# RWKV-7 recurrence of a hybrid decoder step: chunk by chunk, or solves and transition matrices in batches

## The chip, the core and the metric

The kernel runs on one core of a Trainium2 chip. The metric is the device time of one execution in microseconds, the median of the runs shown. TensorE (PE) multiplies, VectorE (DVE), ScalarE (ACT) and GpSimd (POOL) do the element-wise work and empty PE's accumulators (PSUM), SyncE (SP) issues most of the transfers. Beside the times there is one profiled execution, whose trace gives every instruction of every engine.

## What is computed

One layer for 256 prompt tokens and 64 sample tokens (8 sequences of 8): a combined projection, three branches, gates, an output projection and a convolutional GLU. The change is in the first branch, twelve heads of 64 with a delta rule per token:

```python
def _wkv7_step(S, inp):
    r, w, k, v, kk, a = inp
    sa = jnp.einsum('bhvk,bhk->bhv', S, -kk)
    S = S * w[:, :, None, :] + sa[..., None] * (kk * a)[:, :, None, :] + v[..., None] * k[:, :, None, :]
    return S, jnp.einsum('bhvk,bhk->bhv', S, r)
```

The outputs o are normalised per head, get a bonus term and a gate and go into the branch's projection. The final states are outputs too, one for the prompt and one for each sample sequence.

## The kernel before

All tokens stand side by side: 320 columns, 256 of the prompt and 64 of the samples. A large product (`step` at L365, `mm3` at L100) multiplies a weight block of 128x128, split into a high and a low part (`wh` cast by ACT at L361, `wl` subtracted by DVE at L362), with the activations, also split, in three matmuls over 320 columns: L101, L102, L103.

The recurrence works on six pairs of heads, `hp` 0 to 5, in ten chunks of 32 tokens: chunks 0 to 7 are the prompt, 8 and 9 hold four sample sequences each. With half a pair on 64 partitions, `early(hp)` (L487) forms decay, keys and queries, the triangular matrices `Tm` (L538), and the transposes `bkT`, `UV`, `arT` (L559 to L583). `inverse(hp)` (L604) inverts the triangular matrices on DVE and writes them to `IT` by way of DRAM. `late(hp)` (L645) does the recurrence proper. It begins with `PT` (L658), the product of the inverse with `arT`. Then `chunk` (L667) runs ten times. Its first burst multiplies `IT` with `UV` (L672) and adds the state's part (L677, for samples L675); ACT copies the result into `UV` (L678, L679). Its second burst forms the state's increment (L686), the outputs (L698) and the outputs' part from the state (L704, for samples L701); POOL scales the old state (L693) and DVE adds (L694). The four products at L722 give the samples' new states. At the end come the two output transfers, the copy of `pso`, and a tail that normalises and gates (L733 to L749).

The order on PE is written by a planner (`pump`, L387) with a clock of its own. In each turn it first lets every thread (`early`, `inverse`, `late`) go on whose delay has passed or whose condition holds, then it emits one `step` of the first large product in the list and moves its clock by 0.405; if no product may run, it moves the clock by 0.2 and emits none. A `yield` of a number is a delay on that clock, a `yield` of a function a condition. On PE the order of the program is kept; the other engines' instructions are ordered by the framework. The delays that matter: `HOP` = 1.2 after each burst of a chunk, `TRS` = 2.4 after batches of transposes, `NI_LAT`, `BLK_LAT` = 6, `IT_LAT` = 8 in the inverse. The conditions: `early(hp)` waits for `state["late"] >= hp - 1` (L515), the transfer into `IT` too (L636), and a `late` for the one before it (L646) and its inverse (L651).

The list of products: 2 low-rank inputs, then for each pair 3 columns (k, r, v) and `FILL` = 3, 2, 3, 2, 2, 2 others, each of 16 steps; then 16 gate columns, which may run only when `early` has reached 6 (L765, L768), because their output takes the place of early's tiles; then the branch's projection, which needs all six pairs' outputs (L782), and the attention stage.

## Time and profile before

| | us |
|---|---|
| runs: median (lowest, highest) of 3 | 2121.61 (2120.63, 2124.82) |
| profiled execution, span | 2120.2 |
| PE busy in the span | 2066.6 |
| stage with recurrence on PE | 170 to 571.5 |

The span is the time from the first to the last instruction of the profiled execution. A busy time is the union of an engine's instructions; matmuls are pipelined, so a PE that is busy throughout can still issue slowly. In a timeline of PE a line like `x4` stands for four records; a product of two f32 operands that are not of the split kind makes two records, one for each pass. The form `64*32` behind MATMUL gives the rows and columns of the array that it uses. Lines with `sm` and `pso` are small products, those with `bigps` large ones. The page's rows on DVE, ACT and POOL give their busy time; idle time of these costs only what PE waits for.

### The profile page before, as it was taken

Reading aid. Unit: us, or ns where it says so; the run is one execution under the profiler, and the core shown is the slowest. Engines: PE = TensorE matmul, PEld = TensorE weight load, DVE = VectorE, ACT = ScalarE, POOL = GpSimd, SP = SyncE. Lnnn points to the kernel's source line nnn. Section 1 sums busy time; section 2 is a strip of 40 time slices with the busy share of each in tenths; the row PEclk is TensorE's granted clock in tenths of the full one; section 3 lists DMA queues with packets and bytes.
Section 4 is the critical chain, followed back from the end, with each engine's and each line's share of the span. In section 5 each row is a group of like instructions: output and inputs, shape, how many; then the busy total and the mean of one; then the engine's idle time right before and its main releaser. Section 6 shows DMA issues by size and latency. Waiting matters only on the chain.

```text
span 2120.2 us, 37224 instructions
## 1 busy us (share of the span) xinstructions
PE 2066.6 (97%) x15250; PEld 1967.7 (93%) x15250; DVE 1224.8 (58%) x2052; ACT 830.2 (39%) x1372; POOL 255.1 (12%) x506
## 2 busy tenths in 40 slices
PE   8999999999999999999999999999999999999996
PEld 7888888878899889999998999999999999999995
DVE  7677667756356665444545754455555455455457
ACT  5543433432243343333444433343333333333234
POOL 4512232232110000000101300000000000000002
PEclk9999999989999999999999999999999999999998
DMA  7533332333265443554544244445444444444443
GB/s 269 170 120 102 116 107 89 106 97 95 86 225 162 134 127 121 157 159 147 195 159 149 97 149 150 149 152 188 150 149 154 150 149 151 149 149 150 149 138 109
DMA packets 92619, 303.39 MB, mean 143 GB/s; under 512 B 11164, under 2 KB 17078, under 8 KB 92432
## 3 DMA queue, kind: packets, MB, share of 16 engines
q1 hardware_dynamic: 83232, 273.49, 39.9%
q0 software_dynamic: 8496, 26.71, 3.9%
q8 instruction: 119, 1.95, 0.4%
q10 hardware_dynamic: 720, 0.82, 0.1%
q14 instruction: 52, 0.43, 0.1%
HBM read 293.59 MB, written 9.34 MB: 143 GB/s over the span
## 4 chain that ended last, share of the span: by engine, by line
PE 92%; DVE 4%; DMA 1%; issue 1%; ACT 1%; POOL 1%; SPq 0%; DVEq 0%; ACTq 0%; POOLq 0%
PE bigps L101 28%; PE bigps L102 26%; PE bigps L103 26%; PE sm L672 1%; PE sm L677 1%; PE sm L675 1%; PE sm L686 1%; PE sm L129 1%; PE sm L150 1%; DMA NI<-sc 1%; PE pso L698 0%; PE sm L590 0%; PE pso L701 0%; PE sm L852 0%; DVE wl L222 0%
## 5 line engine op out<-in xcount | busy, mean ns | idle before, releaser
L101 PE MATMUL bigps<-XH,wh 128*128 128x320 f32 x2680 | 856.3, 320 | 2.6 <-ACT XH L1069 1.7
L102 PE MATMUL bigps<-XL,wh 128*128 128x320 f32 x2680 | 830.5, 310 | 2.3 <-POOL XL L262 1.5
L103 PE MATMUL bigps<-XH,wl 128*128 128x320 f32 x2680 | 830.5, 310 | 2.1 <-DVE wl L362 2.1
L101 PEld LDWEIGHTS bigps<-XH,wh 128*128 128x128 f32 x2680 | 505.3, 189 | 18.2 <-issue 4.6
L97 DVE TENSOR_TENSOR wl<-raw,wh 128x1024 fp32r<-128x1024 f32 (+1 forms) x299 | 359.5, 1203 | 275.1 <-ACT wh L96 274.6
L102 PEld LDWEIGHTS bigps<-XL,wh 128*128 128x128 f32 x2680 | 505.8, 189 | 5.2 <-POOL XL L262 2.4
L96 ACT CAST wh<-raw 128x1024 fp32r<-128x1024 f32 (+1 forms) x299 | 306.3, 1025 | 517.3 <-PE bigps L102 406.5
L103 PEld LDWEIGHTS bigps<-XH,wl 128*128 128x128 f32 x2680 | 505.2, 188 | 2.6 <-DVE wl L362 2.6
L362 DVE TENSOR_TENSOR wl<-raw,wh 128x1024 fp32r<-128x1024 f32 (+2 forms) x212 | 243.2, 1148 | 180.9 <-ACT wh L361 179.5
L361 ACT CAST wh<-raw 128x1024 fp32r<-128x1024 f32 (+2 forms) x212 | 208.3, 983 | 329.8 <-PE bigps L102 259.3
L102 PE MATMUL bigps<-fl,wh 128*128 128x320 f32 x704 | 217.4, 309 | 0.0
L101 PE MATMUL bigps<-fh,wh 128*128 128x320 f32 x704 | 217.4, 309 | 0.0
L103 PE MATMUL bigps<-fh,wl 128*128 128x320 f32 x704 | 217.3, 309 | 0.0
L101 PEld LDWEIGHTS bigps<-fh,wh 128*128 128x128 f32 x704 | 132.1, 188 | 0.2 <-ACT fh L155 0.2
L102 PEld LDWEIGHTS bigps<-fl,wh 128*128 128x128 f32 x704 | 132.1, 188 | 0.1
L103 PEld LDWEIGHTS bigps<-fh,wl 128*128 128x128 f32 x704 | 132.1, 188 | 0.0
L1115 POOL COPY cout<-zp 128x9 f32<-128x9 f32 x88 | 16.5, 218 | 743.5 <-DVE zp L1112 743.5
L1141 DVE TENSOR_TENSOR yacc<-yacc,bigps 128x320 f32<-128x320 f32 x80 | 38.9, 487 | 84.6 <-PE bigps L103 84.5
L101 PE MATMUL bigps<-MG,wh 128*128 128x320 f32 x208 | 64.3, 309 | 0.0
L102 PE MATMUL bigps<-MG,wh 128*128 128x320 f32 x208 | 64.3, 309 | 0.0
L103 PE MATMUL bigps<-MG,wl 128*128 128x320 f32 x208 | 64.2, 309 | 0.0
L693 POOL TENSOR_SCALAR SP<-S,pc 128x64 f32<-128x64 f32 x42 | 36.3, 865 | 171.2 <-DVE S L694 144.4
(391 smaller groups left out, 2531.4 us busy)
## 6 DMA issues: line engine op xcount, KB each, us to landing
raw<-in_wup SPq DMA_DIRECT2D x176, 512.0 KB, 3.5
raw<-in_win SPq DMA_DIRECT2D x164, 512.0 KB, 3.6
raw<-in_wdn SPq DMA_DIRECT2D x80, 512.0 KB, 3.4
raw<-in_wo SPq DMA_DIRECT2D x32, 512.0 KB, 3.5
raw<-in_wbr_rw SPq DMA_DIRECT2D x16, 384.0 KB, 3.4
raw<-in_wbr_sw SPq DMA_DIRECT2D x16, 384.0 KB, 3.4
ck<-in_cmk POOLq DMA_DIRECT2D x8, 512.0 KB, 4.5
cv<-in_cmv POOLq DMA_DIRECT2D x8, 512.0 KB, 4.7
```

The source lines that it names most:

```text
L96: A.copy(out=h, in_=raw)
L97: V.tensor_sub(out=l, in0=raw, in1=h.bitcast(F32))
L101: PE.matmul(ps, h, xh, start=start, stop=False)
L102: PE.matmul(ps, h, xl, start=False, stop=False)
L103: PE.matmul(ps, l, xh, start=False, stop=stop)
L129: mm = PE.matmul(pst[:, nh * j:nh * j + nh], sq_[:, t0:t0 + 128], rhs, start=q == 0, stop=q == len(sqs) - 1)
L150: PE.matmul(ps[:, n:n + c1 - c0], lhs, C["ident"][:, c0:c1], start=True, stop=True)
L361: A.copy(out=h, in_=c[2])
L362: V.tensor_sub(out=l, in0=c[2], in1=h.bitcast(F32))
L672: PE.matmul(psu[us, 0:64], IT[us, c, :], UV[us, c, :], start=True, stop=c == 0)
L693: G.tensor_scalar(out=SP, in0=S, scalar1=pcc, scalar2=None, op0=ALU.mult)
L1141: V.tensor_add(out=yacc[:, m, :], in0=yacc[:, m, :], in1=ps)
```

## The change

The chunk loop goes. For a pair of heads, `late` now runs: (1) four matmuls for the samples' transition and the solves `IT` times [`arT` | `UV`] for chunks 8, 9 and 0 to 3, 128 columns at a time, (2) the solves of chunks 4 to 7 and the samples' state part, (3) for each chunk the product that gives its state transition (`AB`, block-diagonal for both heads, with the identity added) and the corrected queries, the state increments of all prompt chunks into one bank `psb`, and the outputs from `UV` into `pso`, (4) a chain of seven matmuls, each `AB` times the state, added in `psb` onto the increment, scaled by ACT into `SA`, (5) one closing group: outputs from the states, and the samples' new states. Delays of `SLV` = 2.4 stand behind (1) and (2), `HOP` behind (3) and between the links of the chain. `Tm` and `bkT` become one tile `BT`, `UV` and `arT` one tile `AU`; `ar` has its two halves exchanged, and the mask's columns follow. The two low-rank products of `early` are taken over all 128 partitions with zeros in the other half. The tail's products move from a bank of their own to the two of `early`. `S2` moves to another pool.

```diff
-ARTB = 1
+SLV = 2.4
...
-            tc.tile_pool(name="pso", bufs=1, space=PSUM) as psop, tc.tile_pool(name="ppo", bufs=1, space=PSUM) as ppo, \
+            tc.tile_pool(name="pso", bufs=1, space=PSUM) as psop, tc.tile_pool(name="psb", bufs=1, space=PSUM) as psbp, \
...
+        lord = rws.tile([128, T], F32, name="lord")
+        G.memset(lord[64:128, :], 0.0)
...
+        its = [rws.tile([128, 11, 32], F32, name=f"IT{j}") for j in range(2)]
...
+        AB = rws.tile([128, 7, 128], F32, name="AB")
+        G.memset(AB, 0.0)
+        PTz = rws.tile([128, 2, 64], F32, name="PTz")
+        G.memset(PTz, 0.0)
...
-                    A.activation(out=lora[0][0:64, :], in_=lora[0][0:64, :], func=AF.Tanh)
+                    A.activation(out=lord[0:64, :], in_=lora[0][0:64, :], func=AF.Tanh)
+                    G.memset(lora[0][0:64, :], 0.0)
...
-            PE.matmul(psz, lw[0:64, 0, cs], lwa[0:64, :], start=True, stop=True)
+            PE.matmul(psz, lw[:, 0, cs], lord, start=True, stop=True)
...
-            PE.matmul(psa, lw[64:128, 0, cs], lwa[64:128, :], start=True, stop=True)
+            PE.matmul(psa, lw[:, 0, cs], lora[0], start=True, stop=True)
...
-            Tm = rwm.tile([128, 10, 64], F32, tag="Tm", name="Tm")
+            BT = rwm.tile([128, 10, 128], F32, tag="BT", name="BT")
...
-            bkT = rwm.tile([128, 10, 64], F32, tag="bkT", name="bkT")
-            UV = rwm.tile([128, 10, 64], F32, tag="UV", name="UV")
-            arT = rwm.tile([128, 10, 64], F32, tag="arT", name="arT", bufs=ARTB)
+            AU = rwm.tile([128, 10, 128], F32, tag="AU", name="AU")
...
+        def late(hp, ar, pc, bonus, BT, it, AU):
             yield lambda: state["late"] == hp
             cs = slice(hp * 128, hp * 128 + 128)
             S0 = rw1.tile([128, 8, 64], F32, tag="S0", name="S0")
             nc.gpsimd.dma_start(out=S0, in_=i["wkv"][hp])
             yield lambda: it[0] is not None
+            ITf = it[0].rearrange("p c t -> p (c t)")
+            fss = [slice(64 * h, 64 * h + 64) for h in range(2)]
+            uss = [slice(64 * h, 64 * h + 32) for h in range(2)]
+
+            def bank():
+                return pch.tile([128, 512], F32, tag="sm", name="sm")
+
+            def solve(ps, lo, hi):
+                for c in range(lo, hi):
+                    for h in range(2):
+                        PE.matmul(ps[fss[h], 128 * (c - lo):128 * (c - lo) + 128], ITf[uss[h], 32 * c:32 * c + 64],
+                                  AU[uss[h], c, :], start=True, stop=True)
+
+            def solved(ps, lo, hi):
+                for h in range(2):
+                    (A.copy if h else V.tensor_copy)(out=AU[uss[h], lo:hi, :],
+                                                     in_=ps[uss[h], 0:128 * (hi - lo)].rearrange("p (c f) -> p c f", f=128))
+
+            ps1, ps2 = bank(), bank()
+            for cc in range(2):
+                for h in range(2):
+                    PE.matmul(ps1[fss[h], 256 + 32 * cc:288 + 32 * cc], AU[uss[h], 8 + cc, 0:64],
+                              it[0][uss[h], 8 + cc, :], start=True, stop=True)
+            solve(ps1, 8, 10)
+            solve(ps2, 0, 4)
+            A.copy(out=PTz[:, :, 0:32], in_=ps1[:, 256:320].rearrange("p (c t) -> p c t", t=32))
+            solved(ps1, 8, 10)
+            solved(ps2, 0, 4)
+            yield SLV
+            ps3 = bank()
+            solve(ps3, 4, 8)
+            solved(ps3, 4, 8)
+            psz = bank()
+            for cc in range(2):
+                for h in range(2):
+                    PE.matmul(psz[fss[h], 256 * cc:256 * cc + 256], PTz[fss[h], cc, :],
+                              S0[fss[h], 4 * cc:4 * cc + 4, :].rearrange("p s v -> p (s v)"), start=True, stop=True)
+            UVm = rw1.tile([128, 2, 4, 64], F32, tag="UVm", name="UVm")
+            V.tensor_add(out=UVm, in0=psz.rearrange("p (c s v) -> p c s v", s=4, v=64),
+                         in1=AU[:, 8:10, 64:128].unsqueeze(2).to_broadcast([128, 2, 4, 64]))
+            G.tensor_mul(out=UVm, in0=UVm, in1=C["smask"].unsqueeze(1).unsqueeze(3).to_broadcast([128, 2, 4, 64]))
+            yield SLV
+            for lo, hi in ((1, 5), (5, 10)):
+                ps = bank()
+                pv = ps[:, 0:480].rearrange("p (c f) -> p c f", f=96)
+                for c in range(lo, hi):
+                    w = 0 if c < 8 else 64
+                    for h in range(2):
+                        PE.matmul(pv[fss[h], c - lo, w:96], AU[uss[h], c, 0:64], BT[uss[h], c, w:96], start=True, stop=True)
+                n = min(hi, 8) - lo
+                for h in range(2):
+                    hs = slice(64 * h, 64 * h + 64)
+                    V.tensor_add(out=AB[hs, lo - 1:lo - 1 + n, hs], in0=pv[hs, 0:n, 0:64],
+                                 in1=C["ident"][hs, hs].unsqueeze(1).to_broadcast([64, n, 64]))
+                qv = ar[:, 0, 32 * lo:32 * hi].rearrange("p (c t) -> p c t", t=32)
+                V.tensor_add(out=qv, in0=pv[:, 0:hi - lo, 64:96], in1=qv)
+            psb = psbp.tile([128, 512], F32, tag="psb", name="psb")
+            pso = psop.tile([128, 512], F32, tag="acc", name="pso")
+            for c in range(8):
+                for h in range(2):
+                    PE.matmul(psb[fss[h], 64 * c:64 * c + 64], BT[fss[h], c, 0:64], AU[fss[h], c, 64:128],
+                              start=c == 0, stop=c == 7, skip_group_check=True)
+            SA = rw1.tile([128, 8, 64], F32, tag="SA", name="SA")
+            A.activation(out=SA[:, 0, :], in_=psb[:, 0:64], func=AF.Copy, scale=pc[:, 0:1])
             for c in range(10):
                 for h in range(2):
+                    PE.matmul(pso[fss[h], 32 * c:32 * c + 32], AU[fss[h], c, 64:128], BT[fss[h], c, 64:96],
+                              start=c == 0, stop=False, skip_group_check=True)
+            yield HOP
+            for c in range(1, 8):
+                PE.matmul(psb[:, 64 * c:64 * c + 64], AB[:, c - 1, :], SA[:, c - 1, :], start=False, stop=True,
+                          skip_group_check=True)
+                A.activation(out=SA[:, c, :], in_=psb[:, 64 * c:64 * c + 64], func=AF.Copy, scale=pc[:, c:c + 1])
+                if c < 7:
+                    yield HOP
+            for c in range(1, 8):
+                for h in range(2):
+                    PE.matmul(pso[fss[h], 32 * c:32 * c + 32], SA[fss[h], c - 1, :], ar[fss[h], 0, 32 * c:32 * c + 32],
+                              start=False, stop=False, skip_group_check=True)
+            for b in range(8):
+                for h in range(2):
+                    oc = slice(TP + 8 * b, TP + 8 * b + 8)
+                    PE.matmul(pso[fss[h], oc], S0[fss[h], b, :], ar[fss[h], 0, oc], start=False, stop=b == 7, skip_group_check=True)
+            pss = bank()
             for cc in range(2):
                 for h in range(2):
+                    PE.matmul(pss[fss[h], 256 * cc:256 * cc + 256], BT[fss[h], 8 + cc, 0:64],
+                              UVm[fss[h], cc].rearrange("p s v -> p (s v)"), start=True, stop=True)
+            V.tensor_add(out=S0, in0=pss.rearrange("p (b v) -> p b v", v=64), in1=S0)
+            G.tensor_mul(out=S0, in0=S0, in1=pc[:, 8:16].unsqueeze(2).to_broadcast([128, 8, 64]))
+            nc.gpsimd.dma_start(out=o["wkvs"][hp], in_=S0)
+            nc.gpsimd.dma_start(out=o["wkvp"][hp], in_=SA[:, 7, :])
             ob = tp()
             A.copy(out=ob, in_=pso[:, :T])
             state["late"] = hp + 1
             yield 2.0
+            psm = pea.tile([128, 512], F32, tag="sm", name="sm")[:, :T]
             PE.matmul(psm, C["bones"], ob, start=True, stop=True)
             V.scalar_tensor_tensor(out=ob, in0=psm, scalar=-1.0 / 64, in1=ob, op0=ALU.mult, op1=ALU.add)
             sq = tp()
             A.activation(out=sq, in_=ob, func=AF.Square)
             yield 3.0
+            ex = rstd(pea, rwm, sq, 2, scale=1.0 / 64, add=6.4e-4)
             yield RST
+            rn = spread(pea, ex, 2)
             V.tensor_mul(out=ob, in0=ob, in1=rn)
             A.activation(out=ob, in_=ob, func=AF.Identity, scale=col("lnw", hp), bias=col("lnb", hp))
             yield 2.0
+            psg = pea.tile([128, 512], F32, tag="sm", name="sm")[:, :T]
             PE.matmul(psg, lw[:, 1, cs], lora[1], start=True, stop=True)
             V.tensor_add(out=ob, in0=ob, in1=bonus)
             V.tensor_mul(out=ob, in0=psg, in1=ob)
```

## Rows read from the trace of the kernel before

**Rows 1.** The page: span, and part 1, busy time and share of each engine.
```profile
span 2120.2 us, 37224 instructions
...
PE 2066.6 (97%) x15250; PEld 1967.7 (93%) x15250; DVE 1224.8 (58%) x2052; ACT 830.2 (39%) x1372; POOL 255.1 (12%) x506
```

**Rows 2.** Windows: length, busy us (instructions) per engine, granted clock, DMA share, GB/s.
```profile
170.00:571.50 401.50, 397.01 (x3708) 337.45 (x3707) 257.37 (x509) 148.83 (x354) 98.74 (x161) 0.97 0.32 98
255.00:270.00 15.00, 15.00 (x161) 11.44 (x159) 13.75 (x27) 6.05 (x14) 3.17 (x2) 1.00 0.23 72
457.10:481.20 24.10, 21.07 (x238) 15.21 (x237) 11.57 (x36) 8.44 (x28) 4.29 (x8) 0.61 0.22 66
1500.00:1600.00 100.00, 100.00 (x684) 100.00 (x683) 54.70 (x82) 38.76 (x48) 3.98 (x28) 1.00 0.45 149
```

**Rows 3.** Waits of PE from 170 to 575 us: total us, times, longest.
```profile
PE sm L590 <- ACT UV L582: 1.1, 1, 1.1
PE sm L686 <- ACT UV L678: 0.8, 1, 0.8
```

**Rows 4.** Timeline of PE, a first burst of a prompt chunk: start, us, instruction, records.
```profile
484.57 0.31 PE L103 MATMUL bigps<-XH,wl 128*128 128x320 f32 x1
484.81 0.29 PE L672 MATMUL sm<-UV,IT 32*32 32x64 f32 x2
485.03 0.30 PE L677 MATMUL sm<-S,PT 64*32 64x64 f32 x2
...
485.96 0.30 PE L102 MATMUL bigps<-XL,wh 128*128 128x320 f32 x1
```

**Rows 5.** Timeline of PE, a second burst of a prompt chunk.
```profile
486.98 0.31 PE L103 MATMUL bigps<-XH,wl 128*128 128x320 f32 x1
487.22 0.33 PE L686 MATMUL sm<-UV,bkT 64*64 64x64 f32 x4
...
487.99 0.30 PE L102 MATMUL bigps<-XL,wh 128*128 128x320 f32 x1
```

**Rows 6.** Timeline of PE, the bursts of a sample chunk, the second followed by L672.
```profile
489.01 0.31 PE L103 MATMUL bigps<-XH,wl 128*128 128x320 f32 x1
...
491.07 0.31 PE L102 MATMUL bigps<-XL,wh 128*128 128x320 f32 x1
...
492.09 0.31 PE L103 MATMUL bigps<-XH,wl 128*128 128x320 f32 x1
...
494.54 0.31 PE L102 MATMUL bigps<-XL,wh 128*128 128x320 f32 x1
```

**Rows 7.** Timeline of PE, the product with the inverse at a late's start.
```profile
170.84 0.31 PE L103 MATMUL bigps<-XH,wl 128*128 128x320 f32 x1
171.08 1.35 PE L658 MATMUL sm<-IT,arT 32*64 32x32 f32 x40
...
172.61 0.31 PE L102 MATMUL bigps<-XL,wh 128*128 128x320 f32 x1
```

**Rows 8.** Timeline of PE around the state product of the samples (L722) and an L672 burst.
```profile
217.00 0.31 PE L103 MATMUL bigps<-XH,wl 128*128 128x320 f32 x1
...
219.40 0.31 PE L102 MATMUL bigps<-XL,wh 128*128 128x320 f32 x1
```

**Rows 9.** Timeline of PE, three transposes among large matmuls.
```profile
118.04 0.31 PE L103 MATMUL bigps<-XH,wl 128*128 128x320 f32 x1
118.19 0.49 PE L577 MATMUL sm<-cst,rkv 128*128 128x128 f32 x3
...
118.66 0.30 PE L102 MATMUL bigps<-XL,wh 128*128 128x320 f32 x1
```

**Rows 10.** Timeline of PE, last and next large matmul around the dry stretch.
```profile
457.03 0.31 PE L103 MATMUL bigps<-XH,wl 128*128 128x320 f32 x1
...
480.64 0.94 PE L101 MATMUL bigps<-XH,wh 128*128 128x320 f32 x1
```

**Rows 11.** The page's part 5: a group of instructions on POOL: busy, mean ns, idle before.
```profile
L693 POOL TENSOR_SCALAR SP<-S,pc 128x64 f32<-128x64 f32 x42 | 36.3, 865 | 171.2 <-DVE S L694 144.4
```

More of the change, by code (lines that the diff above doesn't have):

```diff
@@ L434, in tile_hybrid_step @@
         lora = [rws.tile([128, T], F32, name=f"lora{j}") for j in range(2)]
-        its = [rws.tile([128, 10, 32], F32, name=f"IT{j}") for j in range(2)]
-        PT = rws.tile([128, 10, 32], F32, name="PT")
+        lord = rws.tile([128, T], F32, name="lord")
+        G.memset(lord[64:128, :], 0.0)
+        its = [rws.tile([128, 11, 32], F32, name=f"IT{j}") for j in range(2)]
+        for j in range(2):
+            G.memset(its[j][:, 10, :], 0.0)
+        AB = rws.tile([128, 7, 128], F32, name="AB")
+        G.memset(AB, 0.0)
+        PTz = rws.tile([128, 2, 64], F32, name="PTz")
+        G.memset(PTz, 0.0)
         def tt():
@@ L488, in early @@
             cs = slice(hp * 128, hp * 128 + 128)
-            lwa = lora[0]
             yield lambda: "lora0" in state
@@ L1023, in tile_hybrid_step @@
     hres = hp_.tile([128, 16, T], F32, name="hres")
+    S2 = hp_.tile([128, T], F32, name="S2")
     wx = ctx.enter_context(ExitStack())
```

101 lines of the change are left out of this document (12 added, 89 removed).

## Prediction

> **What bounds the kernel now.** I read the page first [rows 1]: TensorE (PE) is busy for 97% of the span, of the others, apart from its own weight loads, none for more than 58%. Then the stretches [rows 2]. In the feed-forward part (1500 to 1600 us) PE issues 684 matmuls in 100 us and never stops: 0.147 us for a matmul of 320 columns, which is the pace at which the large products run wherever nothing disturbs them. In the recurrence stage (170 to 571.5 us) it looks just as busy (397 of 401.5 us), but the records there are mixed: large matmuls with bursts of small ones between them. A busy PE does not say what a burst costs. So I price a burst by its gap: from the start of the last large matmul before it to the start of the second large one after it, less two times 0.147. What PE waits for is small: in 170 to 575 us the waits of PE sum to 4.4 us in seven rows, of which the two longest are shown [rows 3]. The kernel is therefore bound by the time that PE needs for its list of matmuls in the order in which the planner put them, and a change of that list is worth what its gaps are worth, unless a wait appears.
>
> **Prices before.** A chunk of the recurrence has two bursts. Burst A (L672, L677, four matmuls, eight records since each f32 product makes two passes) goes from 484.57 to 485.96: 1.39 - 0.29 = 1.10 us [rows 4]. Burst B (L686, L698, L704, six matmuls, twelve records) goes from 486.98 to 487.99: 0.72 us [rows 5]. Fewer records cost more, and the starts say why: in A the tile of the array changes from 32*32 to 64*32 and back, and groups of two records start 0.22 us apart, while in B all tiles are 64*64. The sample chunks: A 2.06 - 0.29 = 1.77 us; B together with a prompt A 2.45 - 0.29 = 2.16, so 1.06 alone [rows 6]. One burst of forty records in one tile form (L658) goes from 170.84 to 172.61: 1.48 us [rows 7]. B and L658 give a line: (1.48 - 0.72) / 28 = 0.027 us for a narrow record (up to 64 columns) and 0.39 us for going in and out of a burst. A then gives a change of form inside a burst: (1.10 - 0.39 - 8 x 0.027) / 3 = 0.16 us. The state product of the samples (L722, eight records of 256 columns, followed by an A) goes from 217.00 to 219.40: 2.40 - 0.29 - 1.10 = 1.01 us [rows 8]. Depending on how much of the 0.39 it carries, a record of 256 columns is 0.08 to 0.12 us; I take 0.107, so 0.053 for 128 columns and 0.040 for 96. A matmul in the full 128*128 form changes no form: three L577 records go from 118.04 to 118.66, 0.33 us or 0.11 each [rows 9].
>
> One head pair before: L658 1.48; chunk 0 with 4 and 8 records 0.50 + 0.60 by the line; seven A 7.7; seven B 5.0; two sample A 3.54; two sample B 2.12; state 1.01. Together 22.0 us, 280 records.
>
> **The batches.** One head pair after, from the diff. First burst: four matmuls of 32 columns (the samples' transition) and twelve solves of 128 columns, all 32*64: 0.39 + 8 x 0.027 + 24 x 0.053 = 1.9. Second: eight solves and four products of 256 columns (64*64): 0.39 + 16 x 0.053 + 0.16 + 8 x 0.107 = 2.25. Third: fourteen matmuls of 96 columns and four of 32, then 16 + 20 narrow ones in 64*64: 0.39 + 28 x 0.040 + 8 x 0.027 + 0.16 + 72 x 0.027 = 3.8. The chain: seven matmuls of 128*128 by 64 columns, two records each, 0.22 us each: 1.55. Closing group: 14 + 16 narrow and four of 256 columns: 0.39 + 60 x 0.027 + 8 x 0.107 = 2.9. Sum 12.4 us, 246 records. Saved per pair 9.6, over six pairs **57.6 us**. All of it is on PE's own queue and PE has no gaps that could absorb it, so it comes off the end. Bounds: with 0.08 and 0.12 for the wide record 12.4 becomes 11.4 to 13.1, so 53 to 64 us.
>
> **The two low-rank products** (L493, L497) become full-height: same columns, no change of form in and out. Removed per pair at most the 0.39 of a burst and one inner change, at least one change: 0.16 to 0.55; I take 0.4, **2.4 us** in all. The zeroing of half of lora[0] is one POOL memset, once, under the 9 planner units that the first pair waits anyway.
>
> **The dry stretch.** From 457.03 to 480.64 PE issues no large matmul [rows 10], and the granted clock falls to 0.61 on average over this stretch [rows 2]. The planner's delays say why. Each large step counts 0.405 units; the 34 products that may run before the gate columns (2 + 18 + 14, 16 steps each) last 220.3 units. The gates need `early` = 6, and early(5) waits at L515 until late(3) is done. A late takes nineteen delays of 1.2, 22.8 units, after its inverse is there. Followed through all six pairs (0.2 a turn when no product is left), late(3) ends at unit 211.8 and early(5) at 237.5: 17 units without a large matmul. After, a late takes 2.4 + 2.4 + 1.2 + 6 x 1.2 = 13.2 units; late(3) ends at 197.2, early(5) at 222.1: under two units. What the stretch costs is not its length but its excess: the small work in it, priced as above, is 15.9 us (of early(5) three batches of 40, 32 and 8 records, 3.4, eleven transposes, 1.2, and with the tail of late(3) two products over 320 columns, 1.1; of late(4) its L658, chunk 0, three A, two B, a sample A and B, 10.2), against 23.6 - 0.15. So 7.5 us, and some half a microsecond of large matmuls on the low clock: 8. I leave 1 us for the two remaining units: **7 us** saved, 0 to 8.
>
> **Waits, old and new.** Of the old ones some 1.5 us stood at hand-offs that go. New: seven hand-offs PE to ACT to PE per pair (a chain step needs the SA that ACT has just scaled), planned 1.2 units apart, three large steps or nine matmuls, 1.3 us. Before, A to B was the same hand-off, with two ACT copies in place of one, at the same distance, and waited 0.8 us at most [rows 3]. Behind a waiting chain matmul the whole PE queue stands, and ACT runs in order, so a weight cast ahead of SA is paid in full. The evictions of the solved batches have 2.4 units. VectorE keeps about as many passes (eight S, PT, UVm and two for S0 go; three copies, UVm, four AB, two for r and one S0 come). It has 257.4 us of work in 401.5 us; with PE some 65 us shorter that is 76%, and 13.75 of 15 us is busy already at 255 to 270 us [rows 2]. If PE needs 4 us less in such a stretch, VectorE is late by up to 2.75 us per pair: 16 us in all as the upper bound for new waits, zero as the lower. I take 5, near the small rows of waits. POOL loses 42 scalings of S, 36 us busy [rows 11], and gets two products over 512 columns per pair that only an output and the closing group wait for. On its queue S0 is now written out at the very end of a late and loaded anew right behind: the load waits for the store, but the next late begins with its inverse, by the planner 20 to 25 units later, so nothing is due. The tail's four products per pair now share two banks with `early`; at the planner's times they come within 1.5 us of a full pair of banks once in six pairs. Nothing for that.
>
> **Sum.** 2120.2 - 57.6 - 2.4 - 7 - 1.5 + 5 = 2056.7 us of span. The median of the runs shown stands 1.4 us above the profiled span, so **2058.1 us**.
>
> **Rivals.** (1) Count, not form: a small matmul has a fixed price. Then a pair costs 22.0 / 280 x 246 = 19.3, six pairs save 16 us, and with the dry stretch and the waits the time is 2120.2 - 16 - 7 + 3.5 + 1.4 = 2102. Against it: 0.027 us a record in L658 [rows 7] beside 0.14 in A [rows 4]. 6%. The Trainium skill, "TensorEngine Tiling (Array Packing)", section Instruction Overhead, speaks for this one: each matmul has an overhead of about 60 cycles, so that one column costs as much as sixty; the forty records of L658 show about that as a floor, but not that A costs no more than it. By that section alone the batches would bring little.
> (2) The clock: the third burst is 3.8 us without a large matmul; the longest shown stretch of small work took the clock down [rows 2, 10]. If it falls once per pair, with 1 to 1.5 us of the burst and some 1 us of large matmuls doubled, that is 15 us: 2073. Against: inside the dry stretch PE also waited, here it issues without a gap. 8%. The Trainium skill, "TensorE: Matmul & The Clock Gate", Part 1, says that activity is what releases the throttle; no run here shows whether a burst of quarter-array matmuls is activity enough.
> (3) The change doesn't shorten the dry stretch, because the inverse and not the late holds early(5): 2065. 7%.
> (4) Slower: the chain. Place: the seven hand-offs of a late, 42 in all. Price: the mean wait of PE there. From 1.6 us a hand-off it eats the whole gain (63.5 us, and the 5 already allowed); 1.8 us gives 2058.1 - 5 + 76 = 2129. It would need ACT to have a weight cast (L361) and another copy ahead of SA each time. Against: ACT is busy for 149 of 401.5 us [rows 2] and no hand-off waited above 1.1 us [rows 3]. 4%.
>
> **How the numbers follow.** Forecast 75%, by its own bounds 2044 to 2070 (57.6 with 53 to 64, waits 0 to 16). With (2) and (3) and half-way sums of them with late weights the range is 2042 to 2080; (1) and (4) lie outside. Faster by over 0.2% (about what a measurement of this kernel can tell from no change): forecast, (1), (2), (3), less a little for what I don't see: 0.93; the same 0.03; slower 0.04.
>
> **What would show it.** Right: each pair has three batches, seven lone 128*128 matmuls and one closing group, gaps of 1.9, 2.3, 3.8, 0.2 and 2.9 us; large matmuls go on until some 2 to 4 us before the gate columns; clock 1.00 through 170 us to the end of the recurrence, which is 65 us earlier; the later stages as long as before. Wrong: waits of PE on ACT for SA or on VectorE for wl of more than a microsecond in each pair; a clock below 1.00 at the third burst; a record in the batches far above 0.03 to 0.05 us.

## The result, and the profile after

The changed kernel takes 2090.1 us, median of 4 executions (2086.4 to 2096.5), against 2123.2 us in the same session: the ratio is 0.9849, 95% interval 0.9828 to 0.987. The forecast was 2058.1 us with a range from 2042 to 2080. So the sign was right, and about half of the 63.5 us that were forecast came (33.1 by the medians).

The profiled execution of the changed kernel is the longest of the four (2096.5 us), 6.4 us above their median; what is read from it stands at the upper end, its waits above all. First its page: the span, PE's busy time and share, and in 40 slices PE's busy share and the granted clock, in tenths.

```profile
span 2094.7 us, 36710 instructions
...
PE 2024.4 (97%) x15046; PEld 1960.5 (94%) x15046; DVE 1230.9 (59%) x2046; ACT 829.1 (40%) x1324; POOL 224.1 (11%) x464
...
PE   8999999989999999999998999999999999999995
...
PEclk9999999999999999999999999999999999999997
```

PE is as busy as before [rows 1] with 42 us less of busy time. Share and slices hide what happened: a 9 stands for anything from 90%, and in the stage of the recurrence (the fourth slice to the eleventh) one single 8 shows. The windows tell more.

The same windows as [rows 2] (length, busy us and instructions of PE, PEld, DVE, ACT, POOL, granted clock, DMA share, GB/s):

```profile
170.00:571.50 401.50, 379.86 (x3686) 352.45 (x3685) 276.00 (x528) 157.97 (x327) 76.42 (x131) 0.95 0.37 114
...
255.00:270.00 15.00, 12.97 (x155) 11.44 (x154) 14.74 (x28) 4.56 (x9) 1.03 (x1) 0.84 0.19 61
```

From 170 to 571.5 us PE was busy for 397.0 of 401.5 us; now it is for 379.9 (the last pair's closing group is done by 540 us, so the end of this window is already another stage). VectorE (DVE) has 276 us of work in the window in place of 257.4, part of it from that next stage. In 255 to 270 us it was busy for 13.75 of 15 us; now for 14.74, while PE is down to 12.97 and the clock to 0.84. The waits of PE in the stage (total us, times, longest), where [rows 3] had none above 1.1 us:

```profile
PE sm L503 <- DVE bonus L604: 5.2, 3, 2.5
PE sm L703 <- ACT AU L670: 3.3, 2, 2.0
PE sm L764 <- DVE BT L553: 3.2, 1, 3.2
PE sm L594 <- ACT AU L586: 2.0, 2, 1.1
PE psb L725 <- ACT SA L718: 1.9, 1, 1.9
PE sm L150 <- DVE rex L142: 1.8, 2, 1.0
PE sm L690 <- ACT AU L670: 1.7, 3, 1.1
```

All waits together are 20.7 us in 160 to 545 us; before, they were 4.4. No single hand-off stands out. In six of these seven rows PE waits until VectorE or ScalarE (ACT) has read a bank of PSUM (L604, L670, L553, L586, L718), to get what was copied or, at L503 and L764, to get the bank free; none waits for a transfer.

**An account of the stage.** Both kernels issue the same large matmuls (those into `bigps` and `psk`), so I cut both at the starts of the 361st and the 2301st of them, 82.1 and 573.4 us before, 80.7 and 548.8 us after. S is the time between the two. W is the part of S in which no matmul runs; "low" the time at 1.2 GHz, of which half, outside W, is counted as lost; net is the rest, that is the time of PE's list at full clock. All are sums over the records of PE and of the clock, in us:

```
                        S      W     low   lost   W+lost   net
before                491.3    8.6   27.3   12.2    20.8   470.5
after                 468.1   26.1   47.8   22.9    49.0   419.1
```

So PE's list became 51.4 us cheaper, and waits with the low clock took 28.2 of it back. Some 6 of these 28 us belong to this one execution: five variants below with nearly the time of the changed kernel (x8_split, x10_ni, x2_gap, x20_pad_noNI, x21_pad48), profiled nearer to their medians, have 38 to 43 us of W+lost in place of 49.0. In before, the dry stretch alone [rows 10] holds 12.1 of the 20.8 us (3.0 idle, and 20.5 us low). It is gone, so outside of it waits and clock went from 8.7 to 49.0 us: 40 us more, some 34 in a typical execution. What follows asks why.

### The profile page after: what moved, and what is told of

It reads as the page before. It is cut to its first block, busy times and chain, and to the rows that moved or that the text cites. A ratio compares the mean times of both kernels' runs of the same rounds, so it can differ in the third digit from the quotient of the medians.

```text
span 2094.7 us, 36710 instructions
## 1 busy us (share of the span) xinstructions
PE 2024.4 (97%) x15046; PEld 1960.5 (94%) x15046; DVE 1230.9 (59%) x2046; ACT 829.1 (40%) x1324; POOL 224.1 (11%) x464
## 4 chain that ended last, share of the span: by engine, by line
PE 84%; DVE 9%; DMA 2%; issue 2%; ACT 2%; POOL 1%; SPq 0%; DVEq 0%; ACTq 0%; POOLq 0%
PE bigps L101 26%; PE bigps L102 25%; PE bigps L103 25%; DVE wl L361 1%; DMA NI<-sc 1%; POOL rsr L138 1%; ACT wh L360 1%; DVE prod L634 1%; PE sm L150 1%; PE sm L129 1%; DMA raw<-in_wup 0%; DVE AU L586 0%; DVE prod L618 0%; PE sm L870 0%; DVE yacc L1174 0%
## 5 line engine op out<-in xcount | busy, mean ns | idle before, releaser
L361 DVE TENSOR_TENSOR wl<-raw,wh 128x1024 fp32r<-128x1024 f32 (+2 forms) x212 | 244.2, 1152 | 189.8 <-ACT wh L360 187.4
L1130 DVE TENSOR_TENSOR zp<-bigps,S 128x256 f32<-128x256 f32 x44 | 18.7, 425 | 57.0 <-PE bigps L103 56.9
```

The costliest lines, as they stand in the source:

```text
L361: V.tensor_sub(out=l, in0=c[2], in1=h.bitcast(F32))
```

## The batches cost what was forecast

Three timelines of PE in the changed kernel (start, us, instruction, tile, shape, records). The first group of a pair:

```profile
310.42 0.31 PE L103 MATMUL bigps<-XH,wl 128*128 128x320 f32 x1
310.66 0.42 PE L676 MATMUL sm<-IT,AU 32*64 32x32 f32 x8
310.92 1.50 PE L665 MATMUL sm<-AU,IT 32*64 32x128 f32 x24
312.35 0.42 PE L101 MATMUL bigps<-XH,wh 128*128 128x320 f32 x1
312.61 0.31 PE L102 MATMUL bigps<-XL,wh 128*128 128x320 f32 x1
```

From 310.42 to 312.61 are 2.19 us, less 0.29: **1.90** (forecast 1.9). The third group of another pair, 108 records:

```profile
258.66 0.31 PE L103 MATMUL bigps<-XH,wl 128*128 128x320 f32 x1
258.90 1.58 PE L703 MATMUL sm<-BT,AU 32*64 32x96 f32 x36
260.40 1.15 PE L715 MATMUL psb<-AU,BT 64*64 64x64 f32 x32
261.39 1.31 PE L721 MATMUL pso<-BT,AU 64*64 64x32 f32 x40
262.62 0.41 PE L101 MATMUL bigps<-XH,wh 128*128 128x320 f32 x1
262.87 0.31 PE L102 MATMUL bigps<-XL,wh 128*128 128x320 f32 x1
```

4.21 - 0.29 = **3.92** (forecast 3.8). The 72 narrow records (L715, L721) start over 2.22 us, 0.031 each; the 36 of L703 over 1.50, 0.042 each. A link of the chain:

```profile
275.55 0.31 PE L103 MATMUL bigps<-XH,wl 128*128 128x320 f32 x1
275.70 0.33 PE L725 MATMUL psb<-SA,AB 128*128 128x64 f32 x2
275.84 0.39 PE L101 MATMUL bigps<-XH,wh 128*128 128x320 f32 x1
276.07 0.31 PE L102 MATMUL bigps<-XL,wh 128*128 128x320 f32 x1
```

0.52 - 0.29 = 0.23 us; of the 34 links that stand alone between large matmuls the median is **0.22** (forecast 0.22). The second group gives 2.23 (2.25), the closing group 2.9 without its chain link (2.9). A pair comes to 12.5 us by these gaps (forecast 12.4). The Trainium skill, "TensorEngine Tiling (Array Packing)", section Instruction Overhead, gives about 60 cycles of overhead for each matmul, however few columns it has. At 2.4 GHz, the clock granted in these rows, that would be 0.025 us (an estimate from the page's figure); the 0.031 us measured here for 32 and 64 columns agree with it as a floor.

## Where the waits come from, in one place

The third group of the next pair is the same list, with a wait before it (in brackets: idle us, and what ended it):

```profile
320.90 0.31 PE L103 MATMUL bigps<-XH,wl 128*128 128x320 f32 x1
323.17 1.58 PE L703 MATMUL sm<-BT,AU 32*64 32x96 f32 x36 [1.96 <-ACT AU L670]
324.68 1.54 PE L715 MATMUL psb<-AU,BT 64*64 64x64 f32 x32
326.00 2.29 PE L721 MATMUL pso<-BT,AU 64*64 64x32 f32 x40
328.23 0.63 PE L101 MATMUL bigps<-XH,wh 128*128 128x320 f32 x1
328.66 0.47 PE L102 MATMUL bigps<-XL,wh 128*128 128x320 f32 x1
328.92 0.47 PE L103 MATMUL bigps<-XH,wl 128*128 128x320 f32 x1
```

PE stood for 1.96 us until L670 on ScalarE had copied the solved batch. From 325.2 to 332 us the clock is then at 1.2 GHz (granted clock 0.50):

```profile
325.20:332.00 6.80, 6.80 (x76) 6.74 (x73) 6.49 (x17) 2.80 (x7) 0.00 (x0) 0.50 0.01 2
```

The 40 records of L721 take 2.23 us where they took 1.23, and the large matmuls start 0.27 us apart, not 0.147. VectorE just before:

```profile
315.23 0.17 DVE L618 TENSOR_TENSOR prod<-rcst,NI 120x4 f32<-120x4 f32 x1 [2.72 <-DMA NI<-sc]
...
319.39 1.21 DVE L361 TENSOR_TENSOR wl<-raw,wh 128x1024 fp32r<-128x1024 f32 x1
...
321.44 0.36 DVE L619 TENSOR_REDUCE rcst<-prod 120x28 f32<-120x196 f32 x1
321.83 0.68 DVE L670 COPY AU<-sm 32x512 f32<-32x512 f32 x1
```

and ScalarE:

```profile
316.34 0.58 ACT L670 COPY AU<-sm 32x512 f32<-32x512 f32 x1 [3.58 <-DVE AU L670]
...
322.54 0.58 ACT L670 COPY AU<-sm 32x512 f32<-32x512 f32 x1 [0.79 <-DVE AU L670]
```

PE was done with that batch by 316.6 us (L665), but VectorE's half of the copy starts at 321.83. Its queue had stood 2.72 us for a transfer (L618 waits for NI) until 315.23, and what the framework had placed ahead of the copy was therefore late: the small triangles of the inverse, other copies, and a weight (L361, 1.21 us). ScalarE's half of the copy starts when VectorE's half ends (idle 3.58 and 0.79 us before L670), so one late engine makes both late.

**The tail's product and a shared bank.** L764, the tail's gate product, comes right behind the products of the triangles (L551), and PE stood for 3.17 us at it, until VectorE had read the triangles' bank (L553, which ran at 438.10 for 0.88 us behind a weight and two other passes):

```profile
438.84 1.44 PE L764 MATMUL sm<-lora,lw 128*128 128x320 f32 x2 [3.17 <-DVE BT L553]
```

In before the same product stands in the same place, has a bank of its own and does not wait:

```profile
236.90 1.38 PE L545 MATMUL sm<-ar,bk 64*64 64x64 f32 x40
238.21 0.81 PE L746 MATMUL sm<-lora,lw 128*128 128x320 f32 x2
```

This wait is in the traces of all variants of the changed kernel, with 0.5 to 6.5 us, and with 5.1 us it is the largest row of the best of them (x19_pad_act_gap). No run gave the tail its own bank back, so what that is worth in time is not shown.

**Waits and clock go together.** In 14 runs of the changed kernel and its variants (all but x8_split, which cuts the group) there are 84 third groups; one without a wait began at the low clock and is left out. Of the 62 without a wait of PE (above 0.25 us in sum, from 4.5 us before to their end), none was followed by a fall of the clock before PE had waited again: in seven the clock fell some 4 us behind the group, each time behind a later wait of 1.8 to 2.1 us. Of the 21 with a wait, 15 were followed by a fall, four of them only after a further wait. In the profiled execution of after, the group at 258.66 is undisturbed, and the ones at 323.17 and 466.26 have a wait and a fall. So a third group (3.9 us of small tiles) without a gap does not lower the clock here; waits of PE beside small work often did. The reverse count says the same: in the 15 traces 98 falls lie in the cut, and ahead of each PE had stood within the last 5 us, 0.8 us or more in 94 of them and about 0.5 us in the other four. The Trainium skill, "TensorE: Matmul & The Clock Gate", Part 1, says that activity is what releases the throttle: the trace agrees in that the clock fell where PE had stood, and the small tiles themselves brought no fall in the 62 groups.

## The experiments

Each was timed beside the kernel before. The account of all of them stands in one table; medians in us, the ratio to before with its 95% interval. The changed kernel itself has 2090.1 us and 0.9849 [0.9828, 0.9870], so a difference of under some 5 us from it is not told from noise. S, W, lost and net come from one profiled execution each.

```
                     median   ratio [95%]                S      W    lost   net
x8_split             2091.5  0.9844 [0.9830, 0.9859]   462.7  23.8   14.4  424.4
x5_inv_after         2082.9  0.9799 [0.9782, 0.9815]   457.8  20.7   18.0  419.1
x6_inv_before        2122.7  0.9993 [0.9983, 1.0003]   491.3   9.7   11.0  470.6
x3_slv               2100.3  0.9887 [0.9872, 0.9901]   470.7  29.7   22.1  418.9
x10_ni               2091.4  0.9845 [0.9826, 0.9865]   463.4  26.4   16.1  420.9
x1_act               2087.2  0.9827 [0.9813, 0.9842]   460.4  23.7   16.7  420.1
x2_gap               2091.2  0.9847 [0.9833, 0.9862]   461.7  26.5   15.9  419.3
x7_lora              2123.9  0.9996 [0.9986, 1.0006]   493.4   9.9   14.2  469.3
x13_noNI_after       2083.5  0.9814 [0.9799, 0.9828]   455.7  22.3   13.1  420.3
x14_noNI_before      2129.0  1.0025 [1.0013, 1.0037]   500.7  13.2   16.8  470.6
x16_dve              2145.9  1.0098 [1.0081, 1.0115]   513.0  55.6   38.1  419.3
x4_pad               2084.7  0.9814 [0.9799, 0.9829]   452.2  23.9    8.3  420.0
x21_pad48            2089.9  0.9840 [0.9821, 0.9860]   461.0  24.7   17.6  418.7
x18_pad_act          2091.0  0.9849 [0.9831, 0.9867]   460.3  27.6   12.1  420.5
x19_pad_act_gap      2077.5  0.9784 [0.9770, 0.9799]   447.1  20.1    7.9  419.1
x20_pad_noNI         2092.1  0.9849 [0.9834, 0.9864]   463.9  28.9   13.9  421.1
x22_unit_after       2096.5  0.9871 [0.9852, 0.9891]   467.8  29.5   20.6  417.7
x23_unit_before      2128.6  1.0026 [1.0011, 1.0040]   502.8  15.1   16.2  471.4
```

The net column is the first finding: 417.7 to 421.1 us in every variant of the changed kernel (424.4 with the third group cut in three), 469.3 to 471.4 in every variant of before. The saving in the list, some 50 us, is there in all of them; what differs is W and lost.

**Is it the dense third group?** (x8_split; the group cut in three)

```diff
                 V.tensor_add(out=qv, in0=pv[:, 0:hi - lo, 64:96], in1=qv)
+                yield 0.8
...
             A.activation(out=SA[:, 0, :], in_=psb[:, 0:64], func=AF.Copy, scale=pc[:, 0:1])
+            yield 0.8
```

> The changed kernel with the third group cut into three, two large steps between the parts (a delay of 0.8 before the increments and of 0.8 before the outputs). Theory 1: the waits come ahead of the groups and stay, so do most of the low stretches: 2086 to 2094. Theory 2: no group is long enough any more to take the clock down, the low clock in the stage falls below 15 us, 2070 to 2078.

2091.5 us, as the changed kernel. W is still 23.8 us, and the list is 5 us dearer, with more groups in it. Less is lost to the clock (14.4 for 22.9 us), but not less than in other variants of the same time with whole groups (13.9 in x20_pad_noNI, 15.9 in x2_gap). With the count of 62 and 21 above, the group's length is not the cause.

**Is it VectorE's load?** The inverse without its block products, in after and, as the control, in before (the inverse is then not the whole inverse, so the first branch gives other numbers, and VectorE has less work).

```diff
-                if b:
+                if False:
```

> The changed kernel without the products between blocks of the inverse (the part of L620 to L632 under `if b:`), so its outputs of the first branch are not the reference's; some 10 us of VectorE work per head pair go, PE's list of matmuls stays. Theory 1 (VectorE and ScalarE reach the copies out of PSUM too late; PE waits, and the clock falls because it waits): PE's waits in the recurrence stage go from 20.7 us to under 6, the stretches on the low clock there from eight to two or fewer, time 2055 to 2065. Theory 2 (the batches of small tiles take the clock down by themselves): waits fall, but the low clock stays for some 30 to 40 us, time 2072 to 2080.

> The same products left out of the kernel before, as a control (outputs of the first branch not the reference's). Theory 1: the kernel before waits 4.4 us in its stage, so it can gain no more than that: 2117 to 2123. Theory 2 says the same. If it gains as much as the changed kernel does, VectorE's load was a bound in both and the forecast's prices of the batches are wrong.

The control is worth nothing (0.9993), in the changed kernel it is worth 7 us: VectorE's work is on PE's path now and was not before. But W is still 20.7 us, where under 6 were expected, and the time lies above both ranges, so this part of VectorE's work is the smaller part of the waits.

**Single hand-offs.** Longer distance behind the solves (x3_slv), other distances of the inverse (x10_ni), both halves of the solved batch copied by ScalarE (x1_act), two units between the pair's start and its first product (x2_gap):

```diff
-SLV = 2.4
+SLV = 4.8
...
-NI_LAT = 6.0
-BLK_LAT = 6.0
+NI_LAT = 10.0
+BLK_LAT = 5.0
...
-                    (A.copy if h else V.tensor_copy)(out=AU[uss[h], lo:hi, :],
+                    A.copy(out=AU[uss[h], lo:hi, :],
...
-            yield E0 if hp == 0 else 0.0
+            yield E0 if hp == 0 else 2.0
```

> The changed kernel with 4.8 instead of 2.4 planner units after the first and the second group (SLV), so that the copies of the solved batches have twice the time; the groups stay as dense. Theory 1: the waits of the third group and of the sample products on AU (some 6 us) and the low stretches behind them go, others (bonus, BT, the transposes' copies) stay: 2076 to 2084. Theory 2: the low clock stays, only the waits go: 2084 to 2088.

> The changed kernel with the inverse's first operations on VectorE placed four units later (NI_LAT 10) and its four block steps one unit closer each (BLK_LAT 5), so the inverse ends at the same unit. Theory 3 (VectorE stands at the head of its in-order queue on the transfer of NI, 16.6 us in the changed kernel, and the copies that PE needs stand behind it): VectorE's wait on NI falls below 6 us, PE's waits at the groups (L665, L690, L703) and on SA, 7.7 us together, fall below 3 with the low stretches behind them, 2076 to 2083. If only the amount of VectorE's work counts: no change, 2087 to 2093.

> The changed kernel with both halves of the solved batches copied out by ScalarE (before: the lower half by VectorE, and ScalarE's copy starts only when VectorE's has ended). Theory 3: the waits on AU at L665, L690 and L703 (5.8 us) and their low stretches go, those on bonus, BT and the transposes' copies stay: 2077 to 2084. If ScalarE is as late as VectorE, nothing is won: 2088 to 2092.

> The changed kernel with a delay of 2 units ahead of the next pair's low-rank products, so that they don't stand behind the bonus product that still holds their bank. Every theory that counts waits: the 5.6 us on L503 and the two low stretches behind them (3.4 us each) go, 2081 to 2085, if no other wait takes their place; if waits only move to the next hand-off, 2087 to 2092.

None gained what its wait was worth. x3_slv is 10 us slower than the changed kernel and outside both ranges: no wait for L670 is left among its rows, those of L594 and L503 rose to 9.7 and 7.3 us (from 2.0 and 5.2). x10_ni and x2_gap changed nothing in the time: in x2_gap the wait of L503 is gone and the chain's (L725) came, 7.7 us; in x10_ni L665 rose to 4.5. x1_act's interval overlaps that of the changed kernel; L703 fell from 3.3 to 1.9 us there, and L725 rose from 1.9 to 6.2.

**The low-rank products alone**, put into the kernel before (x7_lora):

```diff
-            PE.matmul(psz, lw[0:64, 0, cs], lwa[0:64, :], start=True, stop=True)
+            PE.matmul(psz, lw[:, 0, cs], lord, start=True, stop=True)
...
-            PE.matmul(psa, lw[64:128, 0, cs], lwa[64:128, :], start=True, stop=True)
+            PE.matmul(psa, lw[:, 0, cs], lora[0], start=True, stop=True)
```

> The kernel before with the full-height low-rank products alone. By the forecast's price 2.4 us less than before (1 to 3.3); by the bursts of the two traces, 2.12 against 1.61 us where they stand together with the bonus product, 3 us less.

0.9996: between -1.3 and +3.0 us saved. The forecast's 2.4 lies inside, and nothing does too.

**The transfers that VectorE stands for.** The inverse on a constant tile, the two transfers that regroup its input left out, in after and in before (the first branch gives other numbers):

```diff
-            sc = dsc.tile([20, 32, 32], F32, tag="sc", name="sc")
...
-            nc.gpsimd.dma_start(out=NI[0:120].rearrange("p j t -> p (j t)"),
...
+            NI = NIc
```

> The changed kernel with the inverse working on a constant tile: the transfers of the triangular matrix to DRAM and back to NI are left out (outputs of the first branch not the reference's), all of VectorE's operations stay. Theory 3 (VectorE's queue stands on the transfer of NI, and PE's copies stand behind it): VectorE's wait on NI is zero, PE's waits in 90 to 560 us fall from 25 to under 10, the low stretches from nine to three or fewer, 2062 to 2072. If the transfer is only one among many delays: waits 15 to 20 us as in the four variants before, 2082 to 2090.

> The same left out of the kernel before (control; outputs of the first branch not the reference's). Theory 3: its one long wait of 4.0 us at L590 at 124 us goes with the 6.8 us of low clock behind it, the rest was hidden: 2115 to 2119. The dry stretch stays.

7 us in the changed kernel (the intervals just touch; the time lies in the rival's range, not in the theory's), nothing gained in before (5 us lost where 5 to 9 were to be won; W and lost are 30.0 us there for 20.8). In the changed kernel all six third groups run undisturbed: L703 and L594 wait no more. What is left from 160 us on (L762 and L506 are L764 and L503 of after):

```profile
PE sm L762 <- DVE BT L556: 3.2, 1, 3.2
PE sm L506 <- DVE bonus L602: 2.3, 2, 2.1
PE sm L129 <- ACT rt L518: 1.9, 2, 1.2
...
PE sm L688 <- ACT AU L668: 0.7, 1, 0.7
```

L762 waits as long as before, L506 half as long; and 9.8 us of waits now lie in 90 to 160 us, in place of 5.0. So VectorE's stand at the transfer is what made L703 wait, and is not what makes the sum.

**VectorE in program order** in this stage (x16_dve; the order that the kernel's text gives, as PE's queue already has it; `MANUAL` holds PE alone):

```diff
-            tc.manual_schedule(engines=MANUAL):
+            tc.manual_schedule(engines=MANUAL | {mybir.EngineType.DVE}):
```

> The changed kernel with VectorE's instructions of the recurrence stage too kept in the order of the program, as PE's are, in place of the order that the framework makes. Theory 4 (the copies are late because of the order on VectorE, not of the amount of its work): the copies come right behind PE's groups, waits under 12 us, 2070 to 2080. If the amount counts, the blocks of the inverse stand in the way just the same: 2088 or more; and the weights' low parts may come late, which would show as waits of L103 on wl.

2145.9 us, slower than before, with the same net. The order on VectorE's queue is worth more than the whole change:

```profile
PE sm L665 <- ACT AU L670: 9.2, 3, 3.5
PE sm L129 <- ACT rp L755: 6.5, 4, 2.0
PE sm L150 <- DVE rex L142: 5.5, 2, 4.9
PE sm L551 <- DVE rp L760: 5.0, 1, 5.0
```

**A late and the next early apart.** 9.6 or 4.8 units at the end of a late (x4_pad, x21_pad48):

```diff
             A.copy(out=ob, in_=pso[:, :T])
+            yield 9.6
             state["late"] = hp + 1
```

> The changed kernel with 9.6 units more at the end of each late, so that it takes the planner as long as before (22.8 units) and early(5) is held as before. By the forecast's step the dry stretch of some 17 units comes back and costs 7 us: about 2097. If the dry stretch is worth more or nothing: 2090 (nothing) to 2105.

> Half the delay at the end of a late, 4.8 units. Theory of crossing work: about half the gain, 2086 to 2088, with four to six stretches of low clock in the stage. Rival (the delay helps because more large matmuls are left for later stages, not by separation): the same as with 9.6 units or nothing, 2085 or 2090.

x4_pad gained 5 us (the intervals just touch) where a loss was expected, although the dry stretch is back (21.2 us without a large matmul, at 436 us). That costs it 7.5 us (4.9 idle, 6.8 low), and everywhere else waits and clock fell from 49.0 to 24.7 us. Half the delay gave nothing that can be told from the changed kernel.

**Do the mends add up?** The 9.6 units with x1_act (x18_pad_act), with x1_act and x2_gap (x19_pad_act_gap), with the constant tile of x13 (x20_pad_noNI).

> The changed kernel with 9.6 units of delay at the end of a late and the solved batches copied by ScalarE for both halves. Theory (the waits come from the work of late and early crossing on VectorE and ScalarE, and the clock falls after waits): the two mends act on different waits and add, 5 and 3 us: 2080 to 2083. Rival (what is left is in the list itself, a refill of PE for each batch): as the delay alone, 2084 to 2086. Second rival (a mended wait only moves to the next hand-off): 2084 to 2090.

> As the run before it, and 2 units of delay between an early's masks and its first product. Theory of crossing work: the wait for the masks goes as well, 2077 to 2082. Rival (the list): 2084 to 2086. Second rival (waits move on): 2084 to 2090.

> The changed kernel with 9.6 units of delay at the end of a late, and the inverse computed on a constant tile, so that the two transfers that regroup its input are left out (the outputs of the first branch are other numbers). Theory of crossing work: VectorE never stands on a transfer and the waits of PE in the stage fall below 15 us: 2074 to 2080. Rival (the list): not under 2083, the larger of the two single effects. If the waits are VectorE's stand on the transfer alone, the delay adds nothing: 2082 to 2084.

They don't: two mends that gave 5 and 3 (the 3 not told from noise), or 5 and 7 us, gave nothing together (2091.0 and 2092.1, far above the ranges of the theory of crossing work); three gave 12.6. So neither "each wait has its own cause" nor "only the list is left" holds. The best of these plans, x19_pad_act_gap, beats both kernels: 0.9784 (0.9770 to 0.9799) of before. Its waits of PE in 160 to 645 us:

```profile
PE sm L765 <- DVE BT L553: 5.1, 4, 1.5
PE psb L725 <- ACT SA L727: 4.2, 4, 1.7
PE psb L725 <- DVE AB L707: 1.8, 1, 1.8
```

The waits for L670 and L604 that led the list of after are not among its first rows any more; the chain's, at most 1.8 us each, came instead, and the tail's wait for the triangles' bank (L765, after's L764) leads.

**Are the planned distances too short?** PE needs less for what lies between two steps, so the same units last less time. Units of a large step: 0.365 for 0.405 in after (all distances a ninth longer), 0.45 in before (a tenth shorter).

```diff
-                clock[0] += 0.405
+                clock[0] += 0.365
```

> The changed kernel with 0.365 instead of 0.405 planner units for a large step, so that a ninth more large matmuls lie in every planned delay; the large matmuls run out some 22 units earlier. Theory (a planned delay lasts less time since PE needs less for what lies in it, and the copies no longer fit): waits of PE in the stage fall from 26 to under 16 us and the low clock with them: 2070 to 2080. Rival (the waits come from the crowding of work behind each batch, whatever the planned distance): 2085 to 2095. Second rival (the earlier end of the large matmuls costs what the delays give back): a longer dry stretch with waits in it, 2090 to 2100.

> The kernel before with 0.45 instead of 0.405 units for a large step: all planned delays a tenth shorter, with the bursts as they were; the dry stretch is about gone, as in the changed kernel. Theory of the shorter delays: waits of PE rise from 9 to some 20 us, and the low clock with them: 2130 to 2145. Rival (the batches themselves make the waits): waits stay at 8 to 13 us, 2115 to 2126; if the dry stretch were worth 7 us, 2113 to 2118.

In before, shorter distances did bring waits (W from 8.6 to 15.1, +5.5 us in all), here of L677 for the state that VectorE has to scale (L690):

```profile
PE sm L677 <- DVE S L690: 6.1, 2, 3.3
```

but longer ones did not take them away in after. There the large matmuls run out early, as the second rival has it, and a dry stretch of 27.8 us holds some 16 us of waits and low clock (5.3 idle). Elsewhere 24.2 us of waits are left, where under 16 were expected, and some 10 us of low clock:

```profile
PE sm L503 <- DVE bonus L604: 12.1, 4, 3.9
PE sm L690 <- ACT AU L670: 3.9, 3, 1.6
```

L503 waits for L604 because the product needs the bank that the bonus is still read from; it took 12.1 us here. So a shorter distance can bring waits, and is not what holds them in the changed kernel. Whether longer distances lower what the clock costs is not told, since the dry stretch came with them.

**What stays open.** In fourteen traces of the changed form without x16_dve, W and lost sum to 28 to 52 us, in five of the earlier form to 21 to 31 us. That reading PSUM too late on VectorE and ScalarE makes these waits is read from the rows, and x5, x13 and x16 show that VectorE's load, its stand at transfers and its order each move them. Which property of the change makes them so many (that a batch hands over 512 columns at once, that two pairs' work meets more often, or that the tail shares the banks of `early`) was not told apart: no run copies a batch in smaller parts, and none gives the tail its bank back.

## Why the prediction was wrong, step by step

- **What bounds the kernel: PE's list.** Right for before; in the changed kernel the list alone no longer sets the time of this stage. VectorE work that is free in before costs 7 us there (x6, x5).
- **Prices before and The batches** (57.6 us, bounds 53 to 64). The new prices are right to some 0.1 us: 1.90, 2.23, 3.92, 0.22, 2.9. So are those of before where a burst stands alone between large matmuls (medians 1.10, 0.71, 1.77, 1.48). The net account gives 51.4 us for the whole list, where 57.6 and 2.4 for the low-rank products were forecast. Of the missing 8.6 us, 3.4 have a place: the forecast priced the small work inside the dry stretch burst by burst at 15.9 us, but there no large matmul lies between its 235 records, and they took 12.5 us at full clock (24.0 us for the stretch, less 3.0 idle and 8.5 lost to the low clock). The other 5 us are not settled.
- **Two low-rank products** (2.4 us). Not told from nothing (x7_lora).
- **Dry stretch** (7 us, 0 to 8). The planner's units were right: no gap of more than 7.3 us between large matmuls is left. Its place held 12.1 us of waits and low clock. The forecast counted the excess over 15.9 us of small work, and counted so it is 8.7 (12.1 - 3.4), just above the 8. But the time that it gave was not kept: x4_pad, with a dry stretch of 21.2 us, is the faster kernel. The sum had the low clock only in the dry stretch.
- **Waits, old and new** (-1.5, +5, upper bound 16). This is the step that failed. W rose by 17.5 us (20.5 outside the dry stretch), just above the bound, and the step knew no price for what follows a wait: outside the dry stretch 20 us more were lost to the low clock (23 where before had lost 3). Together waits and clock outside the dry stretch cost 40 us, some 34 in a typical execution, where 3.5 were allowed. The reason for the bound was named (VectorE at 13.75 of 15 us), but only the amount of its work was counted, and 5 of the 16 us taken. What the rows show is its order: each copy of a batch is one long instruction on each of two engines that follow one another, in a queue with the next pair's inverse and its stand at a transfer. The tail's products on the banks of `early` were put at nothing; L764 waits 3.2 us there. Of the other parts of this step: on POOL nothing was due, as forecast; the weight cast before SA, feared for the chain, is not what the chain met (one wait of 1.9 us in 42 hand-offs, with ScalarE standing for VectorE's half of L586 just before).
- **Sum.** 63.5 us were forecast in the stage; S fell by 23.2 = 51.4 + 12.1 - 40.3, and the span by 25.5. The list and the dry stretch together gave 63.5 us where 67 were forecast, so the miss is the waits and the clock behind them. The medians differ by 33.1 us; the profiled execution of the changed kernel is 6.4 us above its median.
- **Rivals.** (1), count and not form: its 2102 is nearest to the result, but the mechanism is refuted by the prices above. (2), the clock at the third burst: no fall at 62 undisturbed groups; refuted as stated. The clock did fall, behind PE's waits. The forecast's ground against (2), that PE issues without a gap, failed where PE waited, and it reckoned clock and waits apart. (3): refuted, the stretch is gone. (4), the chain: 1.9 us in all, not 1.6 a hand-off.
- The Trainium skill, "TensorEngine Tiling (Array Packing)", section PSUM Bottleneck, warns that copies out of PSUM may become the bottleneck once tiling has made TensorE faster. The rows of waits agree in kind (20.7 us for 4.4, six of the seven rows shown on readers of PSUM); the forecast did not weigh it.

## What to carry over

A saving on the engine that bounds is worth its list only as long as the next engine's hand-offs keep up: when PE's list in a stage gets a tenth shorter, look for the in-order queue that hands its results back, and price each new wait with the low clock that may follow it. Test a single hand-off's mend against a second plan before believing it: here mends of 5 and 7 us vanished when joined, and three joined gave 12.6 us. When two parts of a kernel come to share PSUM banks, look for a product right behind the other part's, as L764. Few large batches save PE time, but each copy is then one long instruction, and in the place shown above both halves were late at once.

## What the hardware showed that was not expected

- Groups of 3.8 us in small tiles did not lower the clock by themselves: 62 of 62 passed without a fall until PE waited again, while 15 of 21 with a PE wait beside them were followed by 1.2 GHz.
- At the low clock a narrow record costs 0.056 us for 0.031 (L721: 2.23 and 1.23 us for 40), and a large matmul 0.27 for 0.147: both are paid nearly double.
- A dry stretch is not of one price: 23.6 us cost 12 us in before, 21.2 us cost 7.5 in x4_pad, where the clock was low for 6.8 us of it in place of 20.5.
